# New shares of the PSUM banks for two attentions, and a corrected account of engine times

## The chip, the cores and the metric

The kernel runs on one core of one Trainium2 chip. The metric is the device time of one execution in microseconds, as the median of several. The five engines of the core are named as the profile names them: PE (TensorE, with PEld for its weight loads), DVE (VectorE), ACT (ScalarE), POOL (GpSimd) and SP (SyncE, which issues the transfers). PE writes its results into PSUM, which has eight banks of 128 partitions by 512 float32 values; ACT and DVE read them from there.

## The reference

A trunk of two layers over 512 tokens of width 1024, in float32. Every sub-layer is followed by `x <- LayerNorm(4**0.25 * x + sublayer(x))`.

- Layer A, differential attention with 8 heads. Each head has two query/key maps of 64 columns, with rotary positions, and one value map of 128 columns. For a block of 128 queries the scores of both maps are masked (chunks of 64, causal), each goes through a softmax, and `a = p0 - lam * p1` weighs the values. The result is RMS-normalised per head, scaled, and goes through an output projection.
- Layer B, attention with 16 heads of 64 columns on keys and values that are projected once from the output of layer A. With 512 tokens the band of nine chunks is all that lies before a query's chunk. A learned bias by clipped distance is added to the scores.
- Each layer ends with a SwiGLU block, 1024 to twice 2816 and back.

## The kernel before

**Arithmetic.** A float32 product is made from operands split into a high and a low part, with three matmuls (high by high, high by low, low by high). ACT makes the high part, DVE or POOL the low part.

**Stages.** Values and the first query/key projections of layer A; attention A woven with the other projections; the output projection; SwiGLU of layer A; then the same for layer B, and SwiGLU of layer B. The two attentions, with what is woven into them, lie at about 46 to 249 us and 664 to 858 us of the span.

**Attention A** (`unit_a`, line 1043) has 32 units: 8 heads by 4 query blocks `qt`. A unit has four steps on PE, each with followers on other engines:

1. `s`: scores of both maps into two banks; DVE adds the mask and keeps the extreme (`masked`, line 887), ACT takes the exponentials with their sums, DVE mixes the two maps into `e`.
2. `at`: transposes of `e` into one bank; ACT copies them out as `aT`.
3. `o`: `aT` times the values into one bank; ACT squares with a sum, POOL takes the root (`pow`), DVE scales the bank out as `sq`.
4. `ot`: the transpose of `sq` into one bank; ACT writes its high part `oTh`, DVE its low part `oTl`.

`attention_a` (line 1102) interleaves units by the list `STEPS`: in round i it issues `s` of unit i, some fill, `o` of unit i-2, `ot` of unit i-3, more fill, and `at` of unit i-1.

**Attention B** (`unit_b`, line 1284) has 32 units too: 8 pairs of heads by 4 query blocks. `s` writes two banks as in A. `at` transposes the normalised `e` of each head into a bank of its own (`pt`, m = 0 and 1); ACT and DVE split it into `pth` and `ptl`. After the four units of a pair `values_b` (line 1328) makes the outputs of both heads, a bank each (`po`); ACT copies half of the bank (`tl`), DVE adds the other half to it (`ot`).

**PSUM.** The pool `psp` has four tags with two banks each: `sm`, `sc0`, `sc1` and `pj`. `bank(tag, name)` (line 174) takes one, `pair(name)` (line 177) one of `sc0` and one of `sc1`. Before the change a unit's scores are a `pair`, so two units of scores can stand at once, and everything else of an attention (`at`, `o`, `ot` in A; both `pt` and both `po` in B) takes from the two banks of `sm`. `pj` holds the projections that are woven in. Which of the two banks of a tag a new tile gets is settled when the program is built; the PE instruction that first writes it waits until the readers of that bank's last tile are done.

**The order of the work** is written out by hand, instruction by instruction, by a planner inside the kernel. It keeps a clock for PE (`clk`), advanced by `mm` and `transpose` (lines 192 and 197), and a free time for each other engine (`Modelled`, line 58), advanced by a fixed cost plus a cost per element. Followers on ACT, DVE and POOL are put on a list with due times (`later`, `chain`) and issued once the planner's PE clock has passed them; a step of a chain is put off while its inputs are more than 150 ns from ready by the account. `weave` (line 243) issues fill between the steps: `FA` and `FB` say how many nanoseconds of it at each place, and where a step's input is not ready by the account, fill is issued until it is. Fill comes in pieces of three matmuls. Each engine then runs its instructions in the order in which they were issued. `settle` (line 234) issues what is still due for a tile: for an operand before it is used, and for the tile that by the account held a bank, two allocations of that tag ago, before the bank is used anew.

Of the kernel before, what the change touches and what calls it, by code (L numbers as in the profile page):

```python
# [45 lines left out]
LATP = 1300.0  # L46
T_DVE = 300.0
SLACK = 150.0
FA = ((750.0, 2250.0, 600.0), (0.0, 0.0, 1150.0), 29, (1100.0, 900.0, 900.0))
STEPS = (("s", 0), ("fill", 0), ("o", 2), ("ot", 3), ("fill", 1), ("fill", 2), ("at", 1))  # L50
PREP_B = 2
STEPS_B = (("s", 0), ("v", 2), ("fill", 1), ("fill", 0), ("prep", 0), ("at", 1), ("fill", 2))
FB = ((1700.0, 1300.0, 0.0), (600.0, 2150.0, 100.0), 12, (2500.0, 0.0, 5050.0))
FBV = 2400.0
POOL_K, POOL_VA, POOL_VB, POOL_QB, POOL_KB = False, True, True, False, True


class Modelled:


    def __init__(self, real, model, fixed, each):
        self.real, self.model, self.fixed, self.each, self.free_at = real, model, fixed, each, 0.0

    def __getattr__(self, op):
        issue = getattr(self.real, op)

        def run(*args, **kwargs):
            tiles = [a for a in (*args, *kwargs.values()) if hasattr(a, "tensor")]
            out = [kwargs.get("out", args[0] if args else None)]
            if "accum_out" in kwargs:  # L70
                out.append(kwargs["accum_out"])
            start = max([self.free_at] + [self.model.ready(a) for a in tiles] + [self.model.unused(a) for a in out])
            self.free_at = start + self.fixed + self.each * max(a.free_size() for a in tiles)
            self.model.done(tiles, out, self.free_at)
            return issue(*args, **kwargs)  # L75

        return run
# [55 lines left out]
def trunk(ctx, tc, x, a_w_qkv, a_lambda, a_subln_g, a_w_o, kv_w, b_w_q, b_rel_bias, b_w_o,  # L133
          ln_g, ln_b, ffn_w_in, ffn_w_out, cos_t, sin_t, out):
    nc = tc.nc
    model = Model()
    act_e = Modelled(nc.scalar, model, 95.0, 0.83)
    vec_e = Modelled(nc.vector, model, 70.0, 1.04)
    pool_e = Modelled(nc.gpsimd, model, 100.0, 2.2)
    load_e = ModelledLoads(nc.sync, model, 950.0, 4 / 360.0)  # L140
    PS = bass.MemoryType.PSUM
# [35 lines left out]
    def pair(name):  # L177
        return [bank(f"sc{i}", f"{name}_{i}") for i in range(2)]

    def passed(out_, ins, ns, start):  # L180
        at = max([clk[0]] + [model.ready(a) for a in ins] + ([model.unused(out_)] if start else []))
        clk[0] = at + ns
        model.done((*ins, out_), (out_,), clk[0], 180.0)
        tick()
# [7 lines left out]
    def mm(out_, lhsT, rhs, start, stop, cost=1.0):  # L192
        settle([name_of(lhsT), name_of(rhs)])
        nc.tensor.matmul(out_, lhsT, rhs, start=start, stop=stop)  # L194
        passed(out_, (lhsT, rhs), cost * (out_.free_size() / 2.4 + 3), start)

    def transpose(out_, in_):
        settle([name_of(in_)])
# [236 lines left out]
    def layer_norm(y, st, g, b, name, done_=None):  # L435

        mv = small.tile([P, 2], F32, tag="mv", name=f"mv_{name}")
        vec_e.bn_aggr(mv, st)
        rs = small.tile([P, 1], F32, tag="rs", name=f"rs_{name}")
        vec_e.tensor_scalar_add(rs, mv[:, 1:2], LN_EPS)  # L440
        pool_e.tensor_tensor(rs, rs, mexp, op=ALU.pow)
        for h in range(2):
            sl = slice(h * HALF, (h + 1) * HALF)
            vec_e.scalar_tensor_tensor(y[:, sl], y[:, sl], mv[:, 0:1], g[:, sl],
                                           op0=ALU.subtract, op1=ALU.mult)
        for h in range(2):
            sl = slice(h * HALF, (h + 1) * HALF)
            vec_e.scalar_tensor_tensor(y[:, sl], y[:, sl], rs, b[:, sl], op0=ALU.mult, op1=ALU.add)
            if done_:
                done_(sl)  # L450

    def project_out(act, nk, get_xres, banks0, lead, held, gate, ln, tr, name, banks_1=None):

        begun = banks_1 is not None  # L460

        def step(h, b, t, k, w_, j):
            ts_ = slice(t * P, (t + 1) * P)
            ah, al = act(h, k)
            token_major(b, ah[:, ts_], al[:, ts_], w_[0][:, j, :], w_[1][:, j, :],
                        k == 0 and not begun, k == nk - 1)
            return True

        def add(h, t, b):
            residual(xres[t], b, h, sts[t])  # L470

        b01 = banks0(0)
        ws = []
        for c in range(lead // 2):
            while not gate(2 * c + 1):
                yield True
            ws.append(take(f"{name}_0_{c}"))
            for j in range(2):
                for t in range(2):
                    yield step(0, b01[t], t, 2 * c + j, ws[c], j)  # L480
        while not gate(-1):
            yield True
        b23 = banks0(1)
        for c in range(lead // 2):
            for j in range(2):
                for t in range(2):
                    yield step(0, b23[t], 2 + t, 2 * c + j, ws[c], j)
            free(f"{name}_0_{c}")
        xres = get_xres()
        for c in range(lead // 2, nk // 2):  # L490
            while not gate(2 * c + 1):
                yield True
            w_ = take(f"{name}_0_{c}")
            for j in range(2):
                for t in range(NT):
                    yield step(0, (b01 + b23)[t], t, 2 * c + j, w_, j)
            free(f"{name}_0_{c}")
        sts = []
        for t in range(NT):
            sts.append(small.tile([P, 2, 6], F32, tag="st", name=f"st_{name}_{t}"))  # L500
        for t in (2, 3, 0, 1) if lead else range(NT):
            add(0, t, (b01 + b23)[t])
        banks = banks_1 or pair(f"{name}_1a") + pair(f"{name}_1b")
        split = (nk - held) // 2
        for c in range(split):
            w_ = take(f"{name}_1_{c}")
            for j in range(2):
                for t in range(NT):
                    yield step(1, banks[t], t, 2 * c + j, w_, j)
            free(f"{name}_1_{c}")  # L510
        ws = []
        for t in range(NT):
            for i in range(held // 2):
                if t == 0:
                    ws.append(take(f"{name}_1_{split + i}"))
                for j in range(2):
                    yield step(1, banks[t], t, 2 * (split + i) + j, ws[i], j)
                if t == NT - 1:
                    free(f"{name}_1_{split + i}")
            add(1, t, banks[t])  # L520
            ln(t, xres[t], sts[t])
            if tr and t in (1, 2):
                tr(t - 1, xres[t - 1])
# [519 lines left out]
    def unit_a(h, qt):  # L1043

        kend = (qt + 1) * P
        n_ = f"{h}_{qt}"
        sc = pair(f"sc_{n_}")
        scores(sc, *qk[h], qt)
        e = new(ap3, 3, [P, 2, HALF], F32, "e", f"e_{n_}")
        nm = ap6.tile([P, 2], F32, tag="nm", name=f"nm_{n_}")  # L1050
# [23 lines left out]
        aT = new(ap2, 2, [P, HALF], F32, "aT", f"aT_{n_}")  # L1074
        chain([aT, pt], (lambda: [pt], lambda: act_e.copy(aT[:, :kend], pt[:, :kend])))
        yield aT
        po = bank("sm", f"o_{n_}")
        for kt in range(qt + 1):
            mm(po[:, 0:P], aT[:, kt * P:(kt + 1) * P], vt[kt][:, h * P:(h + 1) * P],
               start=(kt == 0), stop=(kt == qt), cost=4.0)  # L1080
        sq = new(ap2, 2, [P, P], F32, "sq", f"sq_{n_}")
        ms = ap6.tile([P, 1], F32, tag="ms", name=f"ms_{n_}")
        rr = ap6.tile([P, 1], F32, tag="rr", name=f"rr_{n_}")

        def root():
            pool_e.tensor_scalar(ms, ms, 1.0 / P, SUBLN_EPS, op0=ALU.mult, op1=ALU.add)
            pool_e.tensor_tensor(rr, ms, mexp, op=ALU.pow)
            pool_e.tensor_tensor(rr, rr, r[:, 0:1], op=ALU.mult)

        chain([sq, po], (lambda: [po], lambda: act_e.activation(  # L1090
# [48 lines left out]
    def o_proj(oh, ol, res_src, l, name):  # L1139
# [7 lines left out]
            return xres  # L1147

        def banks0(i):
            if i == 0:  # L1150
                return [bank("pj", f"{name}_0_{j}") for j in range(2)]
            return pair(f"{name}_0_23")

        def gate(k):
            return done["s"] if k < 0 else done["o"] >= k
# [128 lines left out]
    def unit_b(p, qt):  # L1284
# [1 line left out]
        bias = biases[p]  # L1286
        kend = (qt + 1) * P
        n_ = f"b{p}_{qt}"
        sc = pair(f"sc_{n_}")
        scores(sc, *qk[p], qt)  # L1290
        e = new(bp2, 2, [P, 2, HALF], F32, "e", f"e_{n_}")
        mx = small.tile([P, 2], F32, tag="nm", name=f"mx_{n_}")
# [17 lines left out]
        yield e  # L1310
        _, pth, ptl = held[p]
        for m in range(2):
            pt = bank("sm", f"pt_{n_}_{m}")
            for kt in range(qt + 1):
                transpose(pt[:, kt * P:(kt + 1) * P], e[:, m, kt * P:(kt + 1) * P])
            dh = pth[m][:, qt * P:qt * P + P]
# [11 lines left out]
    def values_b(p):  # L1328
# [1 line left out]
        ot = new(bp2, 2, [P, S], F32, "ot", f"ot_{p}")  # L1330
        steps, used = [], [ot, oTh, oTl]
        for m in range(2):
            po = bank("sm", f"po_{p}_{m}")
            for kt, lo in ((0, 0), (1, 128), (2, 256), (3, 256)):
                for i, src in enumerate((pth[m], ptl[m])):
                    mm(po[:, lo:S], vs[:, kt, m, :, :].rearrange("p a e -> p (a e)"),
                       src[:, kt * KOFF + lo:kt * KOFF + S],
                       start=(kt == 0 and i == 0), stop=(kt == NT - 1 and i == 1))
            tl = new(bp2, 2, [64, S], F32, "tl", f"tl_{p}_{m}")
            used += [po, tl]  # L1340
            steps += [(lambda po=po: [po], lambda tl=tl, po=po: act_e.copy(tl, po[64:P, :])),
                      (lambda tl=tl: [tl], lambda m=m, tl=tl, po=po: vec_e.tensor_add(
                          ot[m * 64:(m + 1) * 64, :], po[0:64, :], tl))]
# [93 lines left out]
```

## Time and profile before

| | us |
|---|---|
| median of 3 runs (1236.62 to 1242.48) | 1239.59 |
| the profiled execution, its own time | 1239.44 |
| its span, from first to last instruction | 1237.7 |
| PE busy in it | 1192.2 (96%) |
| PE weight loads busy | 1078.5 (87%) |
| DVE busy | 834.9 (67%) |
| ACT busy | 556.3 (45%) |
| POOL busy | 405.5 (33%) |
| chain that ended last, share on PE | 86% |

The busy share says how much of the span an engine worked. The mean granted clock of PE was 0.99 of full speed. A row of waits says which engine stood still, before an operation on which tile, until which engine had finished which tile, with the total, the number of times and the longest. A timeline row has the start, the length, the engine, the line, the operation, out<-in, the shape and the count, and in brackets the idle time before it with what ended it. Matmuls overlap: the next starts before the one before it has ended.

### The profile page before, as it was taken

To read this page: it belongs to the slowest core of one execution; us is meant where nothing else is said; L and a number is where in the kernel's file an instruction comes from. 1 tells how busy PE (TensorE), PEld (TensorE's weight loads), DVE (VectorE), ACT (ScalarE), POOL (GpSimd) and SP (SyncE) were. 2 spreads that over 40 slices of the span, in tenths; PEclk is the share of its full clock that TensorE was granted. 3 is DMA by queue.
4 is the path that set the end of the run, shared out by engine and by line. 5 is a ranking of instruction groups with operands and counts; after the bars stand their busy time and mean duration, and the time that the engine had idled before them with its cause. 6 is when DMAs were issued, how large, how long until landed. Compare 5 with 4: busy or idle time off the path is not lost.

```text
span 1237.7 us, 19979 instructions
## 1 busy us (share of the span) xinstructions
PE 1192.2 (96%) x7640; PEld 1078.5 (87%) x7640; DVE 834.9 (67%) x1451; ACT 556.3 (45%) x1049; POOL 405.5 (33%) x410
## 2 busy tenths in 40 slices
PE   8989989899999999999999999989999999999997
PEld 7867877788999999888887888978899999998886
DVE  4677777388678888533465767675888888883327
ACT  4556666425444444322145667663454444443220
POOL 1134343421555564000323233214136666620022
PEclk9999999899999999999999999999999999999999
DMA  8433342245544443533344342335433333353311
GB/s 265 124 89 95 87 110 86 76 153 145 153 139 138 138 124 104 187 98 124 102 119 116 98 120 65 107 94 170 135 98 108 103 103 103 103 176 114 102 68 69
DMA packets 164191, 145.74 MB, mean 118 GB/s; under 512 B 6096, under 2 KB 137456, under 8 KB 164096
## 3 DMA queue, kind: packets, MB, share of 16 engines
q1 hardware_dynamic: 164096, 144.47, 38.6%
q8 instruction: 60, 0.98, 0.3%
q14 instruction: 35, 0.29, 0.1%
HBM read 127.63 MB, written 13.67 MB: 114 GB/s over the span
## 4 chain that ended last, share of the span: by engine, by line
PE 86%; DVE 7%; ACT 3%; issue 2%; DMA 1%; POOL 1%; SPq 0%; DVEq 0%; ACTq 0%; POOLq 0%
PE m L194 31%; PE c L194 5%; PE a L194 5%; PE b L194 5%; PE gu L194 5%; PE d L194 4%; PE vb_ps L194 4%; PE bk_ps L194 3%; PE bq_ps L194 3%; PE va_ps L194 3%; PE q_ps L194 2%; PE k_ps L194 2%; PE sc_b L194 2%; PE po L194 2%; PE pt_b L199 2%
## 5 line engine op out<-in xcount | busy, mean ns | idle before, releaser
L75 ACT ACTIVATE sg<-sg 128x512 f32<-128x512 f32 x38 | 24.1, 633 | 194.8 <-DVE sg L75 194.8
L75 POOL TENSOR_TENSOR sums<-raw_u 128x512 f32<-128x512 f32 x38 | 49.0, 1291 | 190.6 <-DVE s3lo L75 173.3
L75 POOL TENSOR_TENSOR lo_fo<-raw_fo,hi_fo 128x1024 fp32r<-128x1024 f32 x8 | 19.2, 2394 | 217.2 <-ACT hi_fo L75 217.2
L75 DVE TENSOR_TENSOR lo_fk<-raw_fk,hi_fk 128x1024 fp32r<-128x1024 f32 x28 | 33.9, 1223 | 66.4 <-ACT hi_fk L75 66.4
L75 POOL TENSOR_TENSOR sums<-raw_g,sums 128x512 f32<-128x512 f32 x38 | 76.6, 2016 | 0.0
L75 DVE TENSOR_TENSOR m<-m,m 128x256 f32<-128x256 f32 x76 | 31.7, 417 | 62.8 <-PE m L194 62.8
L75 ACT CAST hi_fk<-raw_fk 128x1024 fp32r<-128x1024 f32 x28 | 29.4, 1052 | 76.0 <-PE d L194 70.9
L75 DVE TENSOR_TENSOR alo<-raw_g,ahi 128x1024 fp32r<-128x1024 f32 x38 | 55.0, 1447 | 0.0
L75 POOL TENSOR_TENSOR sums<-sums,raw_g 128x512 f32<-128x512 f32 x38 | 49.8, 1311 | 3.9 <-DMA raw_g<-in_ffn_w_in_dram 1.1
L75 POOL TENSOR_TENSOR sums<-raw_g,raw_u 128x512 f32<-128x512 f32 x38 | 50.1, 1319 | 0.0
L75 DVE TENSOR_TENSOR s1lo<-sums,s1hi 128x1024 fp32r<-128x1024 f32 x38 | 46.0, 1211 | 0.0
L75 DVE TENSOR_TENSOR s3lo<-sums,s3hi 128x1024 fp32r<-128x1024 f32 x38 | 46.0, 1211 | 0.0
L75 ACT CAST hi_fo<-raw_fo 128x1024 fp32r<-128x1024 f32 x16 | 16.9, 1055 | 64.5 <-PE d L194 64.5
L194 PE MATMUL m<-T1h,s1hi 128*128 128x256 f32 x152 | 43.0, 283 | 0.0
L194 PE MATMUL m<-T1l,s1hi 128*128 128x256 f32 x152 | 43.0, 283 | 0.0
L194 PE MATMUL m<-T1h,s1lo 128*128 128x256 f32 x152 | 43.0, 283 | 0.0
L194 PE MATMUL m<-T2g,s1hi 128*128 128x256 f32 x152 | 43.0, 283 | 0.0
L194 PE MATMUL m<-T2b,s1hi 128*128 128x256 f32 x152 | 43.0, 283 | 0.0
L194 PE MATMUL m<-T2g,s1lo 128*128 128x256 f32 x152 | 43.0, 283 | 0.0
L194 PE MATMUL m<-T3h,s3hi 128*128 128x256 f32 x152 | 43.0, 283 | 0.0
L194 PE MATMUL m<-T3l,s3hi 128*128 128x256 f32 x152 | 43.0, 283 | 0.0
L194 PE MATMUL m<-T3h,s3lo 128*128 128x256 f32 x152 | 43.0, 283 | 0.0
(612 smaller groups left out, 4761.6 us busy)
## 6 DMA issues: line engine op xcount, KB each, us to landing
raw_g<-in_ffn_w_in_dram SPq DMA_DIRECT2D x44, 512.0 KB, 3.9
raw_u<-in_ffn_w_in_dram SPq DMA_DIRECT2D x44, 512.0 KB, 5.1
raw_fk<-in_ffn_w_out_dram SPq DMA_DIRECT2D x28, 512.0 KB, 3.6
raw_fo<-in_ffn_w_out_dram SPq DMA_DIRECT2D x16, 512.0 KB, 3.7
skew<-extd SPq DMA_DIRECT2D x16, 320.0 KB, 6.0
raw_va<-in_a_w_qkv_dram SPq DMA_DIRECT2D x8, 512.0 KB, 4.2
raw_q<-in_a_w_qkv_dram SPq DMA_DIRECT2D x8, 512.0 KB, 5.1
raw_k<-in_a_w_qkv_dram SPq DMA_DIRECT2D x8, 512.0 KB, 4.1
```

The lines of the kernel that those rows point to most:

```text
L75: return issue(*args, **kwargs)
L194: nc.tensor.matmul(out_, lhsT, rhs, start=start, stop=stop)
L199: nc.tensor.transpose(out_, in_, ident)
```

## The change

All attention tiles keep their sizes and their operations; which tag they take changes, and so do numbers of the account. No instruction is added or removed.

- Scores of a unit take both banks of `sc0` (`twice`), in A and B.
- In A, `o` moves from `sm` to `sc1`; `at` and `ot` stay in `sm`. In B, of `pt` and of `po` the second head's (m = 1) moves to `sc1`.
- The output projections take their banks accordingly: token blocks 2 and 3 of the first half from `sc0`; for the second half blocks 0 and 1 from `sc1`, and 2 and 3 from `sc0`.
- The account: a matmul costs 10 ns more, an ACT instruction 15 ns and a DVE one 10 ns more; an instruction with a sum as a second output costs 180 ns more on ACT and 30 ns more on DVE; POOL's `pow` costs 700 ns more in the layer norms and 350 ns more in attention A. The factor for the matmuls of `o` goes from 4.0 to 3.4. The fill rates `FA`, `FB` and `FBV` rise by 4 to 5%.

```diff
-FA = ((750.0, 2250.0, 600.0), (0.0, 0.0, 1150.0), 29, (1100.0, 900.0, 900.0))
+FA = ((780.0, 2350.0, 630.0), (0.0, 0.0, 1200.0), 29, (1150.0, 940.0, 940.0))
-FB = ((1700.0, 1300.0, 0.0), (600.0, 2150.0, 100.0), 12, (2500.0, 0.0, 5050.0))
-FBV = 2400.0
+FB = ((1780.0, 1360.0, 0.0), (630.0, 2250.0, 100.0), 12, (2600.0, 0.0, 5250.0))
+FBV = 2500.0
...
-        def run(*args, **kwargs):
+        def run(*args, more=0.0, **kwargs):
...
                 out.append(kwargs["accum_out"])
+                more += self.read
...
-            self.free_at = start + self.fixed + self.each * max(a.free_size() for a in tiles)
+            self.free_at = start + self.fixed + more + self.each * max(a.free_size() for a in tiles)
...
-    act_e = Modelled(nc.scalar, model, 95.0, 0.83)
-    vec_e = Modelled(nc.vector, model, 70.0, 1.04)
+    act_e = Modelled(nc.scalar, model, 110.0, 0.83, 180.0)
+    vec_e = Modelled(nc.vector, model, 80.0, 1.04, 30.0)
...
+    def twice(tag, name):
+        return [bank(tag, f"{name}_{i}") for i in range(2)]
...
-        passed(out_, (lhsT, rhs), cost * (out_.free_size() / 2.4 + 3), start)
+        passed(out_, (lhsT, rhs), cost * (out_.free_size() / 2.4 + 13), start)
...
-        pool_e.tensor_tensor(rs, rs, mexp, op=ALU.pow)
+        pool_e.tensor_tensor(rs, rs, mexp, op=ALU.pow, more=700.0)
...
-        banks = banks_1 or pair(f"{name}_1a") + pair(f"{name}_1b")
+        banks = banks_1 or twice("sc1", f"{name}_1a") + twice("sc0", f"{name}_1b")
...
-        sc = pair(f"sc_{n_}")
+        sc = twice("sc0", f"sc_{n_}")
...
-        po = bank("sm", f"o_{n_}")
+        po = bank("sc1", f"o_{n_}")
...
-               start=(kt == 0), stop=(kt == qt), cost=4.0)
+               start=(kt == 0), stop=(kt == qt), cost=3.4)
...
-            pool_e.tensor_tensor(rr, ms, mexp, op=ALU.pow)
+            pool_e.tensor_tensor(rr, ms, mexp, op=ALU.pow, more=350.0)
...
-            if i == 0:
-                return [bank("pj", f"{name}_0_{j}") for j in range(2)]
-            return pair(f"{name}_0_23")
+            return twice("sc0" if i else "pj", f"{name}_0_{i}")
...
-        sc = pair(f"sc_{n_}")
+        sc = twice("sc0", f"sc_{n_}")
...
-            pt = bank("sm", f"pt_{n_}_{m}")
+            pt = bank(("sm", "sc1")[m], f"pt_{n_}_{m}")
...
-            po = bank("sm", f"po_{p}_{m}")
+            po = bank(("sm", "sc1")[m], f"po_{p}_{m}")
```

## Rows read from the trace of the kernel before

**Rows 1.** Busy time by stretch: us, each engine (instructions), PE clock, DMA share, GB/s

```profile
46.00:232.00 186.00, 167.45 (x938) 141.46 (x937) 136.85 (x352) 111.02 (x312) 63.06 (x105) 0.96 0.32 87
...
312.50:503.00 190.50, 190.50 (x1599) 190.46 (x1598) 152.97 (x207) 84.20 (x113) 96.66 (x70) 1.00 0.46 135
...
sum 1237.70, PE 1192.19 PEld 1078.49 DVE 834.95 ACT 556.32 POOL 405.51; mean PE 85.16 PEld 77.03 DVE 59.64 ACT 39.74 POOL 28.96
```

**Rows 2.** Waits of PE, 46 to 232 us (attention A): total us, times, longest

```profile
PE at L199 <- DVE oTl L75: 12.5, 12, 3.7
PE o L194 <- ACT aT L75: 3.4, 3, 2.5
PE sc L194 <- DMA ks<-ks: 1.9, 2, 1.8
PE at L199 <- DVE sq L75: 0.3, 1, 0.3
```

**Rows 3.** Waits of PE, 664 to 844 us (attention B)

```profile
PE pt_b L199 <- DVE ot L75: 3.2, 5, 1.0
PE ob L194 <- DVE klb_b L75: 2.1, 1, 2.1
PE pt_b L199 <- DVE e_b L75: 1.6, 1, 1.6
PE pt_b L199 <- DVE ptl L75: 0.9, 2, 0.7
```

**Rows 4.** Timeline of PE, three of the twelve waits before `at`

```profile
77.79 0.66 PE L199 MATMUL at<-ident,e 128*128 128x128 f32 x4 [1.37 <-DVE oTl L75]
...
84.30 0.33 PE L199 MATMUL at<-ident,e 128*128 128x128 f32 x1 [3.70 <-DVE oTl L75]
...
221.18 1.11 PE L199 MATMUL at<-ident,e 128*128 128x128 f32 x4 [0.88 <-DVE oTl L75]
```

**Rows 5.** Timeline of DVE around the first two of these waits

```profile
77.44 0.29 DVE L75 TENSOR_TENSOR oTl<-ot,oTh 128x128 fp32r<-128x128 f32 x1
78.40 0.35 DVE L75 SCALAR_TENSOR_TENSOR sq<-o,rr,gsub 128x128 f32<-128x128 f32 x1 [0.67 <-POOL rr L75]
...
79.71 0.35 DVE L75 SCALAR_TENSOR_TENSOR e<-e,c 128x128 f32<-128x128 f32 x1
...
83.56 0.48 DVE L75 SCALAR_TENSOR_TENSOR e<-e,c 128x256 f32<-128x256 f32 x1
```

**Rows 6.** Busy time by stretch, where PE's granted clock was low in attention A

```profile
84.30:89.10 4.80, 4.80 (x18) 3.87 (x19) 2.86 (x10) 2.14 (x9) 1.28 (x5) 0.64 0.01 3
214.90:232.10 17.20, 12.38 (x54) 9.87 (x52) 10.32 (x36) 7.76 (x27) 2.80 (x9) 0.71 0.11 29
```

**Rows 7.** Timeline of PE: first score matmul of a unit, in A and in B

```profile
120.09 0.36 PE L194 MATMUL sc<-ks,qs 128*128 128x256 f32 x1
...
669.85 0.42 PE L194 MATMUL sc_b<-bks,bqs 128*128 128x384 f32 x1
```

**Rows 8.** Timeline of DVE: last reading of the scores of the unit before those

```profile
117.25 0.69 DVE L75 CUSTOM_DVE_ANT_0 e<-sc,mask 128x512 f32<-128x512 f32 x1
...
670.02 0.42 DVE L75 CUSTOM_DVE_ANT_0 e_b<-sc_b,bias 128x256 f32<-128x256 f32 x1
```

**Rows 9.** Timelines of POOL, DVE, ACT and PE, 160 to 165 us

```profile
160.12 2.53 POOL L75 TENSOR_TENSOR lo_va<-raw_va,hi_va 128x1024 fp32r<-128x1024 f32 x1
160.51 2.68 DVE L75 TENSOR_TENSOR krc<-krc,ksw 128x512 f32<-128x512 f32 x1
...
163.23 1.26 ACT L75 CAST ks<-krc 64x512 fp32r<-64x512 f32 x2 [3.19 <-DVE krc L75]
...
164.93 0.71 PE L194 MATMUL o<-va,aT 128*128 128x128 f32 x4 [2.55 <-ACT aT L75]
```

**Rows 10.** Groups by line or tile: busy us, mean ns; or shortest/median/longest ns

```profile
L75 POOL TENSOR_TENSOR rr<-ms,mexp 128x1 f32<-128x1 f32 x32 | 21.5, 671 | 2.7
...
L75 ACT COPY aT<-at x32: 266/418/589, 54.9 to 239.1; 128x128 f32<-128x128 f32 x8, 128x256 f32<-128x256 f32 x8, 128x384 f32<-128x384 f32 x8, 128x512 f32<-128x512 f32 x8
```

More of the change, by code (lines that the diff above doesn't have):

```diff
@@ L52, with __init__ @@
 STEPS_B = (("s", 0), ("v", 2), ("fill", 1), ("fill", 0), ("prep", 0), ("at", 1), ("fill", 2))
-FB = ((1700.0, 1300.0, 0.0), (600.0, 2150.0, 100.0), 12, (2500.0, 0.0, 5050.0))
-FBV = 2400.0
+FB = ((1780.0, 1360.0, 0.0), (630.0, 2250.0, 100.0), 12, (2600.0, 0.0, 5250.0))
+FBV = 2500.0
 POOL_K, POOL_VA, POOL_VB, POOL_QB, POOL_KB = False, True, True, False, True
 class Modelled:
-    def __init__(self, real, model, fixed, each):
-        self.real, self.model, self.fixed, self.each, self.free_at = real, model, fixed, each, 0.0
+    def __init__(self, real, model, fixed, each, read=0.0):
+        self.real, self.model, self.fixed, self.each, self.read, self.free_at = real, model, fixed, each, read, 0.0
     def __getattr__(self, op):
         issue = getattr(self.real, op)
-        def run(*args, **kwargs):
+        def run(*args, more=0.0, **kwargs):
             tiles = [a for a in (*args, *kwargs.values()) if hasattr(a, "tensor")]
```

## The prediction

> **What bounds the kernel now.** I read the busy time by stretch first. PE is busy 1192.2 of 1237.7 us, so it stands idle for 45.5 us in all, and no change of order can win much more than that. In SwiGLU it is busy 190.50 of 190.50 us, in attention A 167.45 of 186 [rows 1]. Then I read PE's waits inside the two attentions. In A it waits 12.5 us in twelve times before `at` for `oTl`, 0.3 for `sq`, 3.4 before `o` for `aT`, and 1.9 before scores for keys [rows 2]. In B it waits 3.2 us before `pt` for `ot`, 0.9 for `ptl`, 1.6 for the exponentials and 2.1 once before the output projection [rows 3]. The four rows on `oTl`, `sq`, `ot` and `ptl` are of one kind: none of these is an operand of the waiting transposes. They are the last readers of the bank that the transposes write. So the end is set by PE, and in the attentions by how soon a bank of `sm` is free: 12.5 + 0.3 + 3.2 + 0.9 = 16.9 us.
>
> Which bank it is can be read too. The `at` at 77.79 starts as `oTl` (77.44, 0.29 long) ends and does not wait for the `sq` at 78.40 [rows 4, 5]. So it took the bank of the `ot` just issued, not that of the `o` two allocations ago, as the planner's account has it: of the two banks the one whose last reader stands first in the program is handed out. The account sees no wait there, and so puts no fill there.
>
> **The banks in A.** With `o` in `sc1`, `sm` serves `at` and `ot` alone. When `at` of unit i-1 asks, one bank has been free since `aT` of unit i-2 was copied, a round earlier, and the `ot` just issued holds the other. So the waits on `oTl` and `sq` go: 12.8 us. What is late next is `at`'s operand `e`. At 84.30 the operand had been mixed at 79.71 + 0.35 = 80.06 [rows 5], over 4 us before, and in the rounds around the other waits I find the mix finished before the wait began too. But this longest one lies where no fill is being issued: `at` would start at about 80.6, and then the next `at` needs the mix at 83.56 + 0.48 = 84.04 [rows 5]. Of its 3.7 us I count half, so 1.8 off.
>
> `o` now has two banks and lets a round pass before either is used again; it did not wait for its bank before, so this is worth nothing.
>
> **The clock.** From 84.30 to 89.10 the granted clock was 0.64 with PE busy throughout, right after the 3.7 us of idleness. At full speed that work needs 4.80 × 0.64 = 3.07 us, so 1.7 come back if the idleness goes. From 214.9 to 232.1 it was 0.71, with PE busy 12.38 of 17.20 us [rows 6]: four units whose fill is used up. There PE follows the other engines. The clock is worth at most 17.2 × 0.29 = 5.0 us and at least nothing; I take 1.0, near the lower end, since the stretch keeps its gaps. Three of the twelve waits lie in it (one is the row at 221.18 [rows 4]). With them gone `o` comes sooner after `at`, with only scores between, and `aT` takes 0.27 to 0.59 us [rows 10]: four times 0.4, so 1.6 off, and 0.7 for one mix that is late.
>
> **The banks in B.** `pt` and `po` of one head share two banks of their own. After `po` of that head the other bank is long free, and the transposes no longer wait for ACT's copy and DVE's add: 3.2 + 0.9 = 4.1 us. FBV's fill follows right behind, as before.
>
> **The price: scores.** Both attentions now have one pair of banks for scores, so every unit waits for DVE's reading of the unit before, where it used to have a round more. Queued behind that wait on PE are `o`, `ot`, `at` and all fill. The trace shows how far off it is. In the worst lag that I find in A, DVE ends reading at 117.25 + 0.69 = 117.94, and the next scores start at 120.09, 2.15 us later. In B I find two units where scores start too early, one at 669.85 against a reading that ends at 670.02 + 0.42 = 670.44 [rows 7, 8]. That is 0.59 at most, less since the second head's matmuls come later; both together 0.5 us. Bounds of this price: nothing, and, if every unit had to wait out one reading, 62 times the 0.5 us of a median reading between the 0.42 and the 0.69 of these rows, so 31 us. I take 0.5, by the nearest rows.
>
> **The account.** It changes the order only. Its old matmul of 256 columns cost 109.7 ns, the new one 119.7; the SwiGLU stretch shows 190.50 / 1599 = 119.1 [rows 1]. POOL's `pow` shows 671 ns [rows 10] where the account had 102, and now has 452. So it moves towards the trace, and fill is put where an operand is really late. The fill rates rise with the price of the fill (3760 against 3600 ns a unit, three matmuls 679 against 649), so the pieces per unit stay at 5.5, and fill runs out at about the same unit. In SwiGLU the due times come some 8% earlier in matmuls, in the same order against each other; the cover is PE without a gap there, with DVE at 152.97 of 190.5 us. If it went, each of 38 rounds would pay; I see nothing that takes it away. What the new order is worth in the attentions the trace can't show. Above, it is the rest of the waits: 3.4 + 1.9 + 1.6 + 2.1 = 9.0 us [rows 2, 3]. Below, it could shuffle the queues into as many new waits as went. I take nothing.
>
> Of these waits one shows its cause. DVE's `krc` took 2.68 us beside POOL's `lo_va` of 2.53, ACT's `ks` waited 3.19 us for it at the head of its queue, `aT` stood behind that, and PE lost 2.55 us [rows 9]. I leave this stall in, since the account has no term for a slow `krc`. The Trainium skill ("SBUF — State Buffer", section "Who interferes with whom") says that a DVE instruction with two inputs in SBUF and a GpSimd instruction that reads SBUF exclude each other for the whole of one of them. By that rule the stall is chance of order and can come back anywhere, and the sum stands as it is; if instead the better account cured it, the sum would be 2.5 us better. The trace agrees with the rule, as the two lie side by side.
>
> **The sum.** A: 12.8 - 1.8 + 1.7 + 1.0 - 1.6 - 0.7 = 11.4. B: 4.1 - 0.5 = 3.6. Together 15.0 us off the profiled execution's own 1239.44, so 1224.4; the median of the runs, 1239.59, is the same within 0.2. I predict 1224 us.
>
> **Rivals.**
>
> *The account wins as well.* The 9.0 us of other waits go too, or most of them, and the tail of A gets its clock back (the other 4.0 us): 1224 - 13 = 1211 at best, about 1214 by the middle. For it: the corrections match the rows. Against it: 2.55 us hang on two engines side by side, and 1.9 on a transfer. It has 0.19.
>
> *The new order gives the gain back.* Every due time moves, and DVE, ACT and POOL run in the order issued. One bad place costs 2 to 4 us (2.55 and 3.70 are the sizes seen [rows 2, 4]); three or four of them eat most of 15 us: 1232 to 1242, about 1237. For it: DVE is busy 136.85 of A's 186 us, so a misplaced instruction is felt. Against it: the account moves towards the measured times. It has 0.21. Here also belongs that the change doesn't do what it says, that banks are handed out otherwise than I read, with the same waits left at 1239.
>
> *Scores become the wait: slower.* The place is the first score matmul of each unit, the price DVE's lag behind PE. It decides once PE gains more on DVE than the distance seen, 2.15 us in the worst round of A. PE is to gain that much on DVE over a few rounds where waits go, and a `krc` of 2.68 us [rows 9] in front of the reading is enough by itself. If every unit waits 0.4 us, 62 transitions cost 25 us: 1224 + 25 = 1249. Against it: 60 of 62 transitions had the reading finished in time, and a wait of PE also lets DVE catch up. It has 0.11.
>
> **How the numbers follow.** The forecast has 0.49 with a range of its own from 1218 to 1231. A measurement of this kernel tells about 0.5% from no change, 6.2 us: faster means below 1233.4, slower above 1245.8. Faster: 0.49 + 0.19 and a fourth of the second rival, 0.05, so 0.73. Slower: the third, and 0.01 of the second, 0.12. Within: 0.15. The range of 8 in 10 runs from 1211, where the first rival ends, to 1241, in the upper part of the second; the third is left out with the last of the second.
>
> **What would show it.** Right: no wait of PE before `at` for `oTl` or `sq`, and none before `pt` for `ot`; `at` waits, if at all, for `e`; scores wait for DVE's reading under 1 us in each attention; A shorter by 10 to 12 us, B by 3 to 4, the SwiGLU stretches as they were; no low clock at 84 us. Wrong: PE waiting before `sc` for DVE in many units, waits for `aT` or keys grown by what the banks gave, or gaps in SwiGLU.

## The result, and the profile after

The changed kernel takes 1221.98 us (median of 4 runs, 1220.81 to 1223.91); the kernel before, run beside it, 1238.11. The ratio is 0.9867 [0.9834, 0.9899]: some 16.5 us faster, with 1224 forecast. The profiled execution took 1223.91 us, with a span of 1222.1.

| | before | after |
|---|---|---|
| span, us | 1237.7 | 1222.1 |
| PE busy | 1192.2 (96%) | 1188.6 (97%) |
| DVE busy | 834.9 (67%) | 834.2 (68%) |
| chain that ended last, share on PE | 86% | 90% |
| attention A with what is woven in, first score matmul to first SwiGLU matmul | 225.9 | 211.8 |
| the same for attention B | 217.5 | 212.5 |
| the two entries of SwiGLU, from its first matmul (`gu`) to the first on `m`, where its main loop starts | 40.0, 38.5 | 40.3, 40.5 |

What lies outside these rows moved by about 1 us, most of it before the first score matmul (46.7 against 47.9), where in the kernels below, which share that code, it lies between 46.4 and 48.7.

The two attention rows come from the busy time by stretch. First the kernel before, over the whole of either attention (the stretch's ends and length; then PE, PEld, DVE, ACT and POOL busy with their instructions; PE's granted clock; DMA share; GB/s):

```profile
46.71:272.65 225.94, 207.38 (x1131) 174.45 (x1130) 161.29 (x399) 124.07 (x337) 78.33 (x121) 0.97 0.35 101
663.88:881.41 217.53, 209.45 (x1198) 182.00 (x1197) 152.15 (x384) 128.40 (x317) 62.60 (x96) 0.99 0.33 105
```

The same view of the changed kernel, with the SwiGLU stretch between the two:

```profile
47.92:259.74 211.82, 203.54 (x1138) 173.67 (x1137) 158.80 (x400) 124.26 (x340) 80.41 (x121) 0.99 0.37 108
299.80:490.20 190.40, 190.40 (x1597) 190.31 (x1596) 157.56 (x207) 85.35 (x113) 108.86 (x72) 1.00 0.47 137
651.33:863.82 212.49, 208.16 (x1199) 182.09 (x1198) 151.01 (x384) 127.78 (x317) 62.78 (x96) 0.99 0.34 107
```

The length of a stretch less PE's busy time is its idleness. In A that fell from 225.94 - 207.38 = 18.6 to 211.82 - 203.54 = 8.3 us, and the busy time itself, for the same matmuls, by 3.8: the clock was 0.99 and not 0.97. In B idleness fell from 8.1 to 4.3 us and busy time by 1.3. SwiGLU is full as before [rows 1]. These are single profiles: a second one of the changed kernel, from its repeat below, has A at 211.92 us with 202.43 busy and B at 212.55, so the lengths hold and the split of A into idleness and clock moves by some 1 us. The executions of one kernel that are compared here lie up to 11 us apart, and below the profile of the banks alone (1228.83, median 1225.52) and that of `o` back in `sm` (1244.66, median 1239.06) are of long ones.

Which waits went is read from the waits of PE in attention A of the changed kernel (total us, times, longest); they answer to [rows 2]:

```profile
PE ot L203 <- DVE sq L76: 2.2, 4, 1.0
PE sc L198 <- DMA ks<-ks: 1.7, 1, 1.7
PE at L203 <- DVE e L76: 1.5, 1, 1.5
PE oa L198 <- DVE nm L76: 1.5, 1, 1.5
PE at L203 <- DVE oTl L76: 1.0, 1, 1.0
```

And in attention B, against [rows 3]:

```profile
PE ob L198 <- DVE klb_b L76: 2.6, 1, 2.6
PE pt_b L203 <- DVE e_b L76: 1.2, 1, 1.2
PE pt_b L203 <- DVE ot L76: 0.3, 1, 0.3
```

Of twelve waits before `at` for `oTl` one is left, and `aT` is waited for no more. In B, `ot` and `ptl` cost 0.3 in place of 4.1 us. No wait before scores for DVE's reading is in either list. Before scores it shows only in the waits of the weight loads, twice in A (0.5 us together) and in five units of B, at 0.3 us or less each:

```profile
PEld sc_b L198 <- DVE mx_b L76: 1.2, 5, 0.3
```

Two waits that are left are for banks too, by the same sign: the tile waited for is no operand of the waiting matmul. Before `oa`, the output projection of A, PE waits until DVE has read the last unit's scores (`nm`), since blocks 2 and 3 now take both banks of `sc0`:

```profile
218.71 0.50 PE L198 MATMUL oa<-hi_oa,oTh 128*128 128x512 f32 x1 [1.46 <-DVE nm L76]
```

Such a wait, 1.3 to 1.7 us, stands in every profile in which all of A has the new banks, and not in the profile before. And `klb_b`, for which `ob` waits 2.6 us in B, is the last reader of a bank of `pj`; that wait was there before, with 2.1 [rows 3].

At the place of the longest old wait, [rows 4] at 84.30, the timeline of PE now has:

```profile
82.88 0.39 PE L198 MATMUL q_ps<-xTh_a,lo_q 128*128 128x512 f32 x1
84.73 0.30 PE L203 MATMUL at<-ident,e 128*128 128x128 f32 x1 [1.46 <-DVE e L76]
```

The 3.70 us for a bank became 1.46 us for the operand `e`, as the prediction had it, and fill stands in front. No low clock follows: of the 5-us slices of A, only the two between 205 and 215 us have one below 0.95 (0.91 and 0.75), where before there were five, at 0.50 to 0.87.

### The profile page after: what moved, and what is told of

Read it like the earlier page. It is cut to its first block, busy times and chain, and to the rows that moved or that the text cites. A ratio compares the mean times of both kernels' runs of the same rounds, so it can differ in the third digit from the quotient of the medians.

```text
span 1222.1 us, 20005 instructions
## 1 busy us (share of the span) xinstructions
PE 1188.6 (97%) x7640; PEld 1079.4 (88%) x7640; DVE 834.2 (68%) x1451; ACT 555.8 (45%) x1049; POOL 417.1 (34%) x410
## 4 chain that ended last, share of the span: by engine, by line
PE 90%; DVE 5%; issue 1%; DMA 1%; ACT 1%; POOL 1%; SPq 0%; DVEq 0%; POOLq 0%; ACTq 0%
PE m L198 31%; PE c L198 5%; PE a L198 5%; PE b L198 5%; PE gu L198 5%; PE d L198 4%; PE va_ps L198 4%; PE vb_ps L198 4%; PE bq_ps L198 3%; PE bk_ps L198 3%; PE q_ps L198 3%; PE k_ps L198 3%; PE ob L198 2%; PE po L198 2%; PE sc_b L198 2%; PE pt_b L203 1%
## 5 line engine op out<-in xcount | busy, mean ns | idle before, releaser
L76 POOL TENSOR_TENSOR sums<-raw_g,sums 128x512 f32<-128x512 f32 x38 | 84.6, 2226 | 0.0
L76 DVE TENSOR_TENSOR alo<-raw_g,ahi 128x1024 fp32r<-128x1024 f32 x38 | 47.0, 1236 | 0.0
L76 ACT CAST s3hi<-sums 128x1024 fp32r<-128x1024 f32 x38 | 40.0, 1052 | 8.3 <-POOL sums L76 4.6
```

## The experiments

Each kernel was timed in five rounds beside the kernel before (medians 1239.96, 1239.13 and 1239.37 us in the three sets); one hundredth of a ratio is 12.4 us.

| | old banks | new banks |
|---|---|---|
| old account | 1 | 0.9887 [0.9862, 0.9912] |
| costs of ACT, DVE and POOL new | 1.0051 [1.0037, 1.0065] | 0.9821 [0.9801, 0.9841] |
| price of matmuls, factor of `o`, fill rates new | not run | 0.9955 [0.9942, 0.9968] |
| both | 1.0074 [1.0056, 1.0092] | 0.9867 [0.9850, 0.9884] |

The third row, called the matmul price below, is the price together with the factor of `o` and the fill rates, which were not taken apart.

**The banks alone.** The tags of the changed kernel, the account of the old one: all tag lines of the diff, none of its numbers. Against the changed kernel:

```diff
...
-    act_e = Modelled(nc.scalar, model, 110.0, 0.83, 180.0)
-    vec_e = Modelled(nc.vector, model, 80.0, 1.04, 30.0)
+    act_e = Modelled(nc.scalar, model, 95.0, 0.83)
+    vec_e = Modelled(nc.vector, model, 70.0, 1.04)
...
-        passed(out_, (lhsT, rhs), cost * (out_.free_size() / 2.4 + 13), start)
+        passed(out_, (lhsT, rhs), cost * (out_.free_size() / 2.4 + 3), start)
...
```

> The new shares of the banks with the old account of engine times. Theory 1 (the banks carry the gain, since transposes no longer wait for the last readers of their bank): 12 to 15 us under the kernel before, ratio 0.988 to 0.991; PE's wait before the transposes of attention A for oTl under 1.5 us in total (12.5 before), before those of B for ot under 0.7 (3.2 before). Theory 2 (the corrected account carries it, by putting fill where operands are late): under 5 us, ratio above 0.996, with new waits before the same transposes for their operands. If both are needed: 5 to 11 us.

Measured: 1225.52 us, 0.9887 [0.9862, 0.9912], so 14.0 us. No wait for `oTl` is left in A and none for `ot` or `ptl` in B. The banks carry the gain. What is late in A is now `aT` (6.3 us in four waits). How one of them comes about is seen in the timelines of POOL, DVE, ACT and PE:

```profile
156.41 2.38 POOL L75 TENSOR_TENSOR lo_va<-raw_va,hi_va 128x1024 fp32r<-128x1024 f32 x1
156.48 2.86 DVE L75 TENSOR_TENSOR krc<-krc,ksw 128x512 f32<-128x512 f32 x1 [0.99 <-POOL ksw L75]
159.38 0.62 ACT L75 CAST ks<-krc 64x512 fp32r<-64x512 f32 x1 [3.61 <-DVE krc L75]
161.08 0.71 PE L197 MATMUL o<-va,aT 128*128 128x128 f32 x4 [2.98 <-ACT aT L75]
```

It is the stall of [rows 9] again: `aT` stands behind `ks` on ACT, and `ks` waits for a `krc` that takes 2.86 us beside `lo_va`. The other long one, 2.85 us at 104.42, stands behind a `ks` that waited 1.90 us for `krc` too. Behind either PE wait the clock falls, as the busy time of two short stretches shows (PE's clock is the third number from the end):

```profile
104.40:109.40 5.00, 4.97 (x13) 4.11 (x14) 2.34 (x7) 2.02 (x5) 3.31 (x3) 0.50 0.38 87
...
161.00:165.00 4.00, 3.92 (x13) 3.21 (x14) 3.87 (x12) 2.05 (x8) 1.07 (x3) 0.61 0.70 187
```

0.50 is 1.2 GHz, the lower of the two levels: five busy microseconds do the work of 2.5.

**The account alone.** The numbers of the changed kernel, the old tags. Against the changed kernel, the tags of both attentions and of the output projections:

```diff
-        sc = twice("sc0", f"sc_{n_}")
+        sc = pair(f"sc_{n_}")
...
-        po = bank("sc1", f"o_{n_}")
+        po = bank("sm", f"o_{n_}")
...
-            pt = bank(("sm", "sc1")[m], f"pt_{n_}_{m}")
+            pt = bank("sm", f"pt_{n_}_{m}")
...
```

> The corrected account with the old shares of the banks. Theory 1: within 4 us of the kernel before, ratio 0.997 to 1.003, and the wait of A's transposes for oTl still 9 to 15 us, since the account still believes another bank than the one handed out. Theory 2: 10 us or more under the kernel before, ratio under 0.992, with that wait under 4 us.

Measured: 1248.94 us, 1.0074 [1.0056, 1.0092]: slower by 9, which I had not expected. A stands at 227.3 us, about where it was, with 10.5 us of waits for `oTl` and 3.8 for `sq` (12.8 together before [rows 2]); B is 223.9 in place of 217.5. PE's waits in B:

```profile
PE pt_b L203 <- DVE ot L76: 6.0, 10, 1.0
PE pt_b L203 <- DVE ptl L76: 3.5, 4, 1.9
```

These two rows were 4.1 us before [rows 3]. On the old banks the better account makes the bank waits worse.

**The scores on one pair, alone.**

```diff
-        sc = pair(f"sc_{n_}")
+        sc = twice("sc0", f"sc_{n_}")
```

> The kernel before with nothing changed but the scores: both banks of one tag for a unit, so each unit waits for the reading of the unit before; everything else still shares the two banks of sm, and the other tag stands empty in the attentions. It prices the change's cost alone. Theory 1: 0 to 2 us over the kernel before, ratio 0.999 to 1.002; PE and its weight loads wait under 3 us in all for the reading. The rival (scores become the wait in many units): 8 us or more over it, ratio above 1.006.

Measured: 1241.17 us, 1.0011 [0.9999, 1.0023], so 1.4 us, from -0.1 to 2.8. The price of the scores alone is as small as the sum had it (0.5). PE's weight loads wait 0.8 us for the reading, in three units of B, and PE itself not at all. The wait before `oa` is not in it, since the output projections keep their old banks here.

**The changed kernel again**, in the set of these three.

> The changed kernel itself, beside the others on one chip, so that its parts can be compared with it: 0.985 to 0.989 of the kernel before by the earlier measurement.

Measured: 1222.82 us, 0.9867 [0.9850, 0.9884], the same ratio as in the first comparison. The account takes 0.0020, some 2.5 us, off the ratio of the banks alone, and the two intervals overlap.

**`o` of A back in `sm`**, all else as changed.

```diff
-        po = bank("sc1", f"o_{n_}")
+        po = bank("sm", f"o_{n_}")
```

> The changed kernel with one line undone: o of attention A takes from sm again, so at, o and ot share two banks; scores, B and the account stay as changed. Theory 1 (the separate banks of o are what frees at): attention A gets longer by 12 to 16 us and B stays, so 1234 to 1239 us, ratio 0.996 to 1.001, and at waits 9 to 15 us for oTl and sq. If the gain of A came from the account: under 4 us longer, ratio under 0.991.

Measured: 1239.06 us, 1.0004 [0.9986, 1.0022], at the upper edge of what was expected. That is 0.0137 or 17.0 us above the changed kernel, from one tag. In A the old waits are back: 10.6 us for `oTl` in eight, and 4.5 us for `sq` in two. B did not move (212.5).

**`pt` and `po` of B back in `sm`**, all else as changed.

```diff
-            pt = bank(("sm", "sc1")[m], f"pt_{n_}_{m}")
+            pt = bank("sm", f"pt_{n_}_{m}")
...
-            po = bank(("sm", "sc1")[m], f"po_{p}_{m}")
+            po = bank("sm", f"po_{p}_{m}")
```

> The changed kernel with the banks of B's transposes and outputs undone: all pt and po from sm. A stays as changed. By the kernel with the corrected account alone, whose attention B was 6 us longer than that of the kernel before: attention B longer by 8 to 12 us, 1230 to 1235 us, ratio 0.992 to 0.997, with pt waiting 8 to 10 us for ot and ptl. By the prediction's sum (4.1 us of waits went): 1226 us, ratio 0.989, with 3 to 5 us of these waits.

Measured: 1233.39 us, 0.9959 [0.9943, 0.9975], as expected, 0.0092 or 11.4 us above the changed kernel; B 224.2 us with 6.1 us of waits for `ot` and 3.5 for `ptl`, as in the account alone. So each of the two moves of banks is worth more under the new account than the waits of before let one read (17.0 and 11.4, against 11.4 and 3.6 in the sum), because the new account on old banks is a worse kernel than the old account on them.

**Which half of the account.** First the new banks with the matmul price, the factor of `o` and the fill rates as before, and the new costs of ACT, DVE and POOL.

```diff
-FA = ((780.0, 2350.0, 630.0), (0.0, 0.0, 1200.0), 29, (1150.0, 940.0, 940.0))
+FA = ((750.0, 2250.0, 600.0), (0.0, 0.0, 1150.0), 29, (1100.0, 900.0, 900.0))
...
-        passed(out_, (lhsT, rhs), cost * (out_.free_size() / 2.4 + 13), start)
+        passed(out_, (lhsT, rhs), cost * (out_.free_size() / 2.4 + 3), start)
```

> The changed kernel with the price of a matmul, the factor for o and the fill rates as before; the higher costs of ACT, DVE and POOL stay. With all of the account as before the new banks gave 1225.5 us, with all of it as changed 1222.8. If the engine costs made the difference (operands that the old account held ready too soon, as aT with 6.3 us of waits before o): 1221 to 1224 us and a wait before o for aT under 1.5 us. If the matmul price made it: 1224.5 to 1227 and over 4 us of that wait.

Measured: 1217.06 us, 0.9821 [0.9801, 0.9841]. It beats the changed kernel by 0.0046 or 5.7 us, which neither theory had; of the first the sign held, with 0.4 us of waits before `o` for `aT` where the banks alone have 6.3. A takes 208.8 us, and the entries of SwiGLU 38.4 each. So the profiles differ by 3.0 us in A and by 3.9 at the entries, and 3.3 of these 3.9 are busy time, that is the clock.

Then the other half alone, on the new banks: the diff above undone, and instead

```diff
-    act_e = Modelled(nc.scalar, model, 110.0, 0.83, 180.0)
-    vec_e = Modelled(nc.vector, model, 80.0, 1.04, 30.0)
+    act_e = Modelled(nc.scalar, model, 95.0, 0.83)
+    vec_e = Modelled(nc.vector, model, 70.0, 1.04)
...
-            pool_e.tensor_tensor(rr, ms, mexp, op=ALU.pow, more=350.0)
+            pool_e.tensor_tensor(rr, ms, mexp, op=ALU.pow)
```

> The new banks with only the matmul price, the factor of o and the fill rates corrected, the other engines' costs as before. Theory (the dearer matmul costs some 5 us wherever it stands, as it does on top of the engine costs): 1225.5 + 5 = 1230, range 1228 to 1233, attention A at 223 us or more. Rival (it costs only together with the engine costs, or by chance of order): 1222 to 1227.

Measured: 1233.99 us, 0.9955 [0.9942, 0.9968]: 0.0068 or 8.4 us worse than the banks with the old account, somewhat beyond the range that its theory gave. A takes 225.3 us, and PE's waits there begin with:

```profile
PE sc L197 <- DMA ks<-ks: 6.4, 2, 5.0
PE o L197 <- ACT aT L75: 4.7, 3, 2.9
```

The 5.0 us stand at 220.76 us, before scores of the last head, whose keys come by a transfer from `ks` to `ks`, issued at 215.85 and landing 4.6 us later. They are made too late. That the dearer matmul makes the followers come late in the order I argue from its place in the account; the run shows only that they do.

And the engine costs on the old banks, that is the tag lines of the account alone with the prices of the first half:

> The banks of before with only the costs of ACT, DVE and POOL corrected; matmul price, factor of o and fill rates as before. The whole account on the old banks was slower by some 9 us. Theory (the dearer matmul with the higher fill rates did that, by making PE's clock in the account run ahead of its bank waits): 1230 to 1239, with the waits before at for oTl at 10 to 13 us and before pt for ot near 3 us, as before. Rival (the costs of the other engines did it): 1245 to 1250, with waits before pt for ot of some 6 us and attention B at 222 us or more. Third (only both together do it): 1237 to 1242.

Measured: 1246.16 us, 1.0051 [1.0037, 1.0065], with B at 224.4 us: the rival was right, and not the theory that put all harm on the matmul price. PE's waits in B have 8.0 us for `ot` in nine, the longest 3.40. Around that one the timelines of ACT, DVE and PE read:

```profile
789.43 1.05 ACT L76 COPY tl<-po 64x512 f32<-64x512 f32 x2
...
786.76 1.39 DVE L76 TENSOR_TENSOR klb_g<-bk_ps,bks 64x512 fp32r<-64x512 f32 x2
788.18 1.23 DVE L76 TENSOR_TENSOR lo_bq<-raw_bq,hi_bq 128x1024 fp32r<-128x1024 f32 x1
789.56 0.17 DVE L76 RECIPROCAL r_b<-s_b 128x2 f32<-128x2 f32 x1
789.76 2.29 DVE L76 TENSOR_SCALAR e_b<-e_b,r_b 128x256 f32<-128x256 f32 x2
792.08 1.40 DVE L76 TENSOR_TENSOR ot<-po,tl 64x512 f32<-64x512 f32 x2
...
792.82 0.47 PE L203 MATMUL pt_b<-ident,e_b 128*128 128x128 f32 x1 [3.40 <-DVE ot L76]
```

PE ended `po` at 789.4. Its banks are free once both `tl` and `ot` have read them; `tl` was done at 790.5, and `ot` stood on DVE until 792.1, behind `r_b` and the two `e_b`. Nothing that these rows write is read by the waiting transposes: they take a block of 128 columns, and the normalisation before `ot` (256 columns) is the next unit's. So what DVE's queue held cost PE 3.40 us because a bank hung on it.

**The entries of SwiGLU.** In the changed kernel PE waits there for a bank of `sm` too, at the last token block. In the timeline of PE:

```profile
269.52 1.40 PE L203 MATMUL xt_ps<-ident,oa_x 128*128 128x128 f32 x8 [1.97 <-ACT hb L76]
...
873.59 1.32 PE L203 MATMUL xt_ps<-ident,ob_x 128*128 128x128 f32 x8 [1.97 <-ACT hb L76]
```

`pj` is idle by then, so the fourth block was given its banks:

```diff
-            pt = bank("sm", f"xt_ps_{t}_{g}")
+            pt = bank("pj" if whole and t == 3 else "sm", f"xt_ps_{t}_{g}")
```

> The changed kernel, with one more bank moved: the last token block's transposes at the start of each SwiGLU take from pj, which stands empty there, and not from sm, whose bank ACT is still copying from (a wait of 1.97 us each time). The wait should go, twice 1.97 us, and with it the stretches of low granted clock behind it, 1.5 us each where they come: 1216 to 1219 us, ratio 0.981 to 0.984. If the copies on ACT bind what follows anyway: no change, 1222 us.

Measured: 1215.31 us, 0.9809 [0.9789, 0.9829], 0.0058 or 7.2 us better than the changed kernel, with both entries at 36.6 us, somewhat better than expected. Of the 7.7 us that the two entries had lost, twice 1.97 is the wait, and 3.7 are busy time: PE does the same work with its clock at 1.00 in place of 0.96.

What makes the wait 1.97 us, where the old account has 1.61 or 1.62? I suspected the 700 ns that the account adds to the `pow` of the layer norms.

```diff
-        pool_e.tensor_tensor(rs, rs, mexp, op=ALU.pow, more=700.0)
+        pool_e.tensor_tensor(rs, rs, mexp, op=ALU.pow)
```

> The changed kernel without the 700 ns that the account adds to POOL's pow in the layer norms. Theory (this term orders the last transposes before each SwiGLU later, which makes PE's wait there 1.97 instead of 1.61 us, and the long wait comes with a granted clock of 0.96 in the 40 us that follow): both waits 1.61 us; if the clock falls only behind the long wait, both entries 38.4 us and 1217.5 to 1219; if it falls by chance behind the short one too, 1219 to 1222. Rival (the term does not order these steps): 1222 with waits of 1.97 us.

Measured: 1222.70 us, 0.9857 [0.9839, 0.9875], and both waits are still 1.97: my suspicion fell. The waits of the other kernels point to the matmul price instead: 1.97 or 1.98 in all seven profiles that have it and the old bank, 1.61 or 1.62 in the five without it. How the price comes to do this was not traced. The busy time by stretch of this kernel's two entries shows something else (clock third from the end):

```profile
257.52:296.27 38.75, 36.43 (x257) 33.70 (x256) 33.20 (x36) 19.46 (x27) 9.48 (x6) 1.00 0.46 129
858.46:898.92 40.46, 38.13 (x257) 35.38 (x256) 32.20 (x36) 19.47 (x27) 7.78 (x6) 0.96 0.43 118
```

The same wait, the same matmuls, once with the full clock and once with 0.96 and 1.7 us more of busy time. So the clock may fall behind this wait and need not. Over all the profiles it was 0.96 at 9 of 14 entries with the wait of 1.97, at 2 of 10 with the one of 1.61, and at none of the 4 where the fourth block has its bank in `pj`. So what the matmul price and the bank of `pj` are worth is in part how often the clock falls there.

**The best version.** Engine costs without the matmul price, and the fourth block in `pj`: the first diff of the halves of the account and the one of the entries together.

> The changed kernel with both improvements found: the matmul price, the factor of o and the fill rates as before the change, and the fourth transposed block of each SwiGLU entry in a bank of pj. Theory (the two act at different places and add up): the two waits of some 1.6 us at the entries of SwiGLU go, each entry takes 36.6 us instead of 38.4, A stays at about 209: 1217.1 - 3.6 = 1213.5, range 1211.5 to 1214.5, ratio 0.979 to 0.981. Rival (of what the pj bank gave in the changed kernel, 6.7 us, most was a clock that no longer fell, and with these prices the clock did not fall anyway): 1215 to 1217.5, entries 38 us.

Measured: 1212.16 us, 0.9787 [0.9769, 0.9805], 26.4 us faster than before and 9.9 faster than the change, inside the range of the theory in time. Both gains stand, but not in full: one by one they were 5.7 and 7.2, 12.9 together. On top of the engine costs the bank of `pj` gives 0.0034 or 4.2 us, about what the entries shorten by (3.7); the clock there, which made up much of its 7.2 us in the changed kernel, does not fall with these prices in either profile. To that extent the rival was right. Its entries:

```profile
256.02:292.57 36.55, 36.20 (x257) 33.75 (x256) 33.78 (x36) 19.43 (x27) 8.77 (x5) 1.00 0.45 124
...
854.46:891.06 36.60, 36.25 (x257) 33.79 (x256) 33.83 (x36) 19.48 (x27) 9.69 (x5) 1.00 0.42 116
```

## Why the prediction was right, and where it was not

**What bounds the kernel.** Right. The waits before `at` and `pt` were waits for banks of `sm`: with other tags and the old account they are gone, and with one tag put back they return. One wait of the kind was read as another: the 2.1 us before `ob`, by the same rule, are for a bank of `pj`, which the change leaves as it was.

**The banks in A.** The sum had 8.7 us of waits (12.8 - 1.8 - 1.6 - 0.7) and 2.7 of clock, 11.4 in all. The stage fell by 14.1: 10.3 of idleness and 3.8 of busy time. Of the busy time the 1.7 at 84 us came back as worked out, so the tail gave some 2, where 1.0 had been taken. The steps went as worked out at 84 us (now a wait for `e`, 1.46 us, no low clock behind it). In the tail, where 2.3 us were taken off for `aT` and the mix, neither is late; what is late there is `sq`, the operand of `ot`, with 1.0 us at 215.78, and the bank of `oa`, 1.46 us. In all, 15.4 us of waits went (11.5 for `oTl`, 3.4 for `aT`, 0.3 for `sq`, 0.2 for keys) and 5.3 came (2.2 before `ot`, 1.5 for `e`, 1.6 before `oa`). Without the 3.4 of `aT`, which the sum had left in, the waits would have fallen by 6.7, less than the 8.7. One wait of 1.0 us for `oTl`, at 120.94, was not foreseen: the claim that one bank has always been free for a round is not true at that place.

**The banks in B.** 3.6 forecast, 5.0 measured: 3.8 of idleness, as worked out, and 1.3 of busy time that I had not counted and cannot place. It is hardly the clock: the stretches where that was low cost about 1.5 us of B before and 1.7 after.

**The scores.** Right in kind and size: 0.5 forecast, 1.4 [-0.1, 2.8] measured alone. In the changed kernel PE does run up to that limit in B, in five units, and stands there 0.3 us at most; this is where the third rival would have begun. What the sum put at nothing is the same price at the output projection of A, the 1.46 us before `oa`.

**The account.** "I take nothing" came out as 2.5 us of gain within overlapping intervals, but only as a sum: on the new banks the engine costs gain 0.0066 or 8.2 us, and the matmul price loses 5.7 of them again. The argument that the price moves towards the measured 119.1 ns and so costs nothing was wrong. So was the step that counts the account apart from the banks: the engine costs lose 6.3 us on the old banks and gain 8.2 on the new.

**The stall at `krc`.** I left it in as chance of order, and that was a term on the wrong side. In the changed kernel it does not occur at this place. The timelines of DVE, POOL and ACT:

```profile
154.76 0.68 DVE L76 TENSOR_TENSOR krc<-krc,ksw 128x512 f32<-128x512 f32 x1
154.87 2.84 POOL L76 TENSOR_TENSOR lo_va<-raw_va,hi_va 128x1024 fp32r<-128x1024 f32 x1 [0.58 <-ACT hi_va L76]
154.68 0.38 ACT L76 COPY aT<-at 128x256 f32<-128x256 f32 x1
155.47 1.26 ACT L76 CAST ks<-krc 64x512 fp32r<-64x512 f32 x2 [0.42 <-DVE krc L76]
```

The same two instructions overlap, but DVE's starts 0.11 us ahead, and takes 0.68 us; in the banks alone POOL's was 0.07 ahead, and DVE's took 2.86. The rule of the Trainium skill ("SBUF — State Buffer", section "Who interferes with whom") that the prediction cited, that the two exclude each other for the whole of one instruction, agrees with both rows. The same section says that the order of issue, not the shape of the operation, decides which of the two is held; these rows show that too, and 0.2 us of start decide on 2.2 us.

A second thing differs: `aT` now stands ahead of `ks` on ACT, so even a slow `krc` would not have held it. In the matmul price alone `krc` does take 2.88 us at 160.81, but `aT` was copied at 159.56, and PE does not wait before `o` there; it waits 1.44 us at 166.76, before scores, for the keys made from this `krc`. So my reading as mere chance does not stand. This `krc` takes 2.68 to 2.88 us in all four kernels without the engine costs and 0.68 or 0.69 in all that have them, and the waits before `o` for `aT` are 3.4 to 6.3 us in the four and 2.4 at most in the others. The account has no term for a slow `krc`, but its new order went with the cure each time, and the first rival was right in this part (3.4 us of waits for `aT` went to none). Why is not shown: some of these orders win by 0.11 us of start or less.

**What cancelled.** Against 15.0 forecast the profiles differ by 15.6: 14.1 and 5.0 gained in the attentions, 2.4 lost at the entries of SwiGLU (0.35 of wait at each, the rest the clock of the second), which the prediction had left out, and about 1 at the start. That 1222 lies so near to 1224 is thus in part luck.

## What to carry to other kernels

A wait before an operation for a tile that it does not read is to be read first as a wait for a buffer, and the next place to look is which tile held that buffer last. Count what such waits cost, and also the clock that falls behind them, for here a quarter to a third of A's gain was clock. A planner's cost table and its buffers have to be changed and tested together: the same correction lost 6.3 us while followers had to free a bank, and gained 8.2 once they did not. When scores give up a bank, look also at what takes their banks after them: here the output projection. A figure brought closer to the measured one is not thereby a better planner; here the best version keeps the old, too low price of a matmul, with the fill rates that go with it.

## What the runs showed of the hardware that I had not expected

- The granted clock behind one and the same wait of 1.97 us was 1.00 at one entry of SwiGLU and 0.96 at the other, 38.75 against 40.46 us. Executions of one kernel differ by it: the six of the banks alone have spans of 1227.4 us at a mean clock of 0.987, and of 1219.1 at 0.996, with the same instructions in the same order.
- Which of two overlapping instructions on DVE and POOL is lengthened hangs on a start 0.1 us earlier or later: 0.68 against 2.86 us for `krc`.
